# Two hybrid attention layers on one core: TensorE order written by hand, heads alternating, value products in long runs

## The chip, the cores and the metric

One core of one Trainium2 chip runs the whole program in one launch. The metric is device time in microseconds (us): the median of several executions. One execution was also profiled, and its trace is what is read below.

TensorE does the matrix products (in the profile PE, its weight loads PEld), VectorE is DVE, ScalarE is ACT, GpSimd is POOL, and SyncE (SP) issues the weight transfers.

## What is computed

A block of sequence length 256 and width 1024, all in float32: a retention/mLSTM mixer, a feed-forward layer and a gated embedding; a sparse attention mixer, a second feed-forward layer and gated embedding; and then two hybrid layers with a last norm. The change is in the hybrid layers. Cut to what matters, such a layer is:

```python
def hybrid_layer(x, mod, ...):
    h = rms_norm_2(x, norm_g) * (1 + scale) + shift
    a_qkv, a_z, m_cq, m_ckv, m_kr, m_z, merge = split(h @ w_in)
    y_a = dilated_mixer(a_qkv, rel_bias) * silu(a_z)          # 8 heads of 64, 3 groups, one softmax over the groups
    y_m = mla_mixer(m_cq, m_ckv, m_kr, ...) * silu(m_z)       # 16 heads, causal, keys of 64 + 32 rotary columns
    g_a, g_m = split(sigmoid(merge))
    return x + gate * ((g_a * (y_a @ w_out_a) + g_m * (y_m @ w_out_b)) @ w_o)
```

## The kernel before

The tokens stand in two blocks of 128 (`tb`). Every weight tile (128 x 1024 floats, 512 KB) goes the same way in `wt`: SyncE issues its transfer into a buffer `raw` (5 of them), ScalarE copies it, rounded, to `whi` (L448), VectorE forms the rest `wlo` (L449), and both of these have 4 buffers. A projection is then three products for each piece of 128 rows (`mm3`, L465 to L467): high by high, high by low, low by high. The line numbers of these three stand for nearly all of TensorE's projections. Their sums are built in three PSUM banks (`acc`, pool `pacc`).

A hybrid layer goes through these parts in program order (`hybrid`):

- the narrow projections and the first group's values (`c_part`, `v_part`), then `quad_in(0, (0,))`, the queries and keys of the first group for heads 0 to 3;
- MLA: values of all 16 heads (`vm`, L1517), then `mla_chunk(0..3)`, four heads each: keys, queries, and for each pair of heads the scores (L1556, contracting over 128 rows), softmax and `pv_pair`;
- `quad_in(0, (1, 2))`, then `quad(0)`: the dilated attention of heads 0 to 3, in two pairs `pr`, each head `e` of a pair in turn; `quad_in(1, ...)`, `quad(1)` for heads 4 to 7;
- the gates `silu_gate` of `mz` and `az`, the merge projections `mg` (L1603), and the output projections.

In a quad the scores of one head (L1465) contract over 64 rows. Head `e` of a pair has rows 0 to 63 or 64 to 127 of the array: the profile writes 64*128. For one head the order in the program is: two groups of 256 keys into one PSUM tile (`sc`, 2 buffers), the third group into the next, and, for the first token block, three groups of 128 keys into another. VectorE adds the bias and takes the extreme value in one instruction (L1468), ScalarE exponentiates (L1473), VectorE scales (L1475).

`pv_pair` takes the probabilities of one group and two heads: three 128 x 128 transposes for each head (L677) into `tp`, a copy to a separate tile `pT` (L682 on ScalarE for one head, L680 on VectorE for the other), then the value products: for each head 256 columns (L685) and 128 columns (L688), into 64 of the 128 partitions of `po`; the profile writes 128*64. So one group of one pair has two products at L685 and two at L688, and the trace records each float32 product of these lines as two passes.

The program order is not the order on the engines. A planner takes all instructions when the program is built and gives each engine its own fixed order by dependences, priorities and estimated costs; so TensorE's order mixes heads, stages and projections freely.

## Time and profile before

| what | value |
|---|---|
| median of 3 executions | 1460.59 us (1460.12 to 1461.44) |
| the profiled execution, its own time | 1459.07 us |
| its span, from first to last instruction | 1457.3 us |
| TensorE busy | 1415.5 us, 97% |
| VectorE busy | 1032.6 us, 71% |
| ScalarE busy | 761.8 us, 52% |
| granted TensorE clock, mean | 0.988 of full speed |

A matmul's time in the profile runs from its start to its modelled end, and matmuls are pipelined: busy time says that something was under way, not that the array was full. What one of them costs its successors is read from one start to the next. The MLA part and the quads with their projections lie at 782 to 968 us in the first hybrid layer and at 1133 to 1319 us in the second.

### The profile page before, as it was taken

To read this page: it belongs to the slowest core of one execution; us is meant where nothing else is said; L and a number is where in the kernel's file an instruction comes from. 1 tells how busy PE (TensorE), PEld (TensorE's weight loads), DVE (VectorE), ACT (ScalarE), POOL (GpSimd) and SP (SyncE) were. 2 spreads that over 40 slices of the span, in tenths; PEclk is the share of its full clock that TensorE was granted. 3 is DMA by queue.
4 is the path that set the end of the run, shared out by engine and by line. 5 is a ranking of instruction groups with operands and counts; after the bars stand their busy time and mean duration, and the time that the engine had idled before them with its cause. 6 is when DMAs were issued, how large, how long until landed. Compare 5 with 4: busy or idle time off the path is not lost.

```text
span 1457.3 us, 23812 instructions
## 1 busy us (share of the span) xinstructions
PE 1415.5 (97%) x9011; PEld 1211.7 (83%) x9011; DVE 1032.6 (71%) x2250; ACT 761.8 (52%) x1383; POOL 56.6 (4%) x89
## 2 busy tenths in 40 slices
PE   8999999999999999999989999999999999999997
PEld 7878999887755699997788888988879787989886
DVE  7678698978777788897677754555577865456466
ACT  6355565446455665553656544444455754344553
POOL 0000000003000000000210011000000102000000
PEclk9999999999979999999999999999999999999999
DMA  7445677875630266687543353525554435434561
GB/s 270 137 144 163 185 246 243 325 281 194 231 110 1 75 216 217 216 293 279 185 142 123 127 167 114 179 83 188 193 192 144 139 110 145 141 124 145 188 209 51
DMA packets 74903, 251.89 MB, mean 173 GB/s; under 512 B 10362, under 2 KB 14498, under 8 KB 74660
## 3 DMA queue, kind: packets, MB, share of 16 engines
q1 hardware_dynamic: 68880, 239.87, 49.1%
q0 software_dynamic: 3840, 6.32, 1.7%
q10 hardware_dynamic: 2068, 4.18, 1.1%
q8 instruction: 71, 1.16, 0.3%
q14 instruction: 44, 0.36, 0.1%
HBM read 248.42 MB, written 1.90 MB: 172 GB/s over the span
## 4 chain that ended last, share of the span: by engine, by line
PE 85%; DVE 6%; ACT 3%; DMA 2%; issue 2%; POOL 1%; SPq 0%; ACTq 0%; DVEq 0%; POOLq 0%
PE acc L465 22%; PE acc L467 22%; PE acc L466 22%; PE po L685 4%; PE tp L677 3%; PE sc L1465 2%; PE sc L1178 2%; DVE wlo L449 2%; ACT whi L448 2%; DMA raw<-weights 1%; PE po L688 1%; PE sc L1556 1%; DMA gb<-rows 1%; POOL rs L631 1%; PE tp L577 1%
## 5 line engine op out<-in xcount | busy, mean ns | idle before, releaser
L449 DVE TENSOR_TENSOR wlo<-raw,whi 128x1024 fp32r<-128x1024 f32 (+2 forms) x386 | 460.1, 1196 | 213.7 <-ACT whi L448 211.5
L448 ACT ACTIVATE whi<-raw 128x1024 fp32r<-128x1024 f32 (+2 forms) x386 | 399.1, 1037 | 335.6 <-PE acc L467 180.3
L465 PE MATMUL acc<-xh,whi 128*128 128x256 f32 (+1 forms) x1360 | 386.7, 285 | 7.1 <-ACT xh L581 4.7
L466 PE MATMUL acc<-xl,whi 128*128 128x256 f32 (+1 forms) x1360 | 388.3, 286 | 0.7 <-DVE xl L582 0.7
L467 PE MATMUL acc<-xh,wlo 128*128 128x256 f32 (+1 forms) x1360 | 386.1, 284 | 0.9 <-DVE wlo L449 0.9
L465 PEld LDWEIGHTS acc<-xh,whi 128*128 128x128 f32 (+1 forms) x1360 | 258.8, 191 | 13.3 <-ACT xh L581 5.7
L466 PEld LDWEIGHTS acc<-xl,whi 128*128 128x128 f32 (+1 forms) x1360 | 259.2, 191 | 6.5 <-issue 4.1
L467 PEld LDWEIGHTS acc<-xh,wlo 128*128 128x128 f32 (+1 forms) x1360 | 259.1, 191 | 2.3 <-DVE wlo L449 1.6
L465 PE MATMUL acc<-whi,xh 128*128 128x512 f32 (+2 forms) x688 | 249.6, 364 | 2.2 <-DVE xh L1354 1.2
L467 PE MATMUL acc<-whi,xl 128*128 128x512 f32 (+2 forms) x688 | 249.2, 363 | 1.3 <-DVE xl L582 1.2
L466 PE MATMUL acc<-wlo,xh 128*128 128x512 f32 (+2 forms) x688 | 248.8, 362 | 0.0
L465 PEld LDWEIGHTS acc<-whi,xh 128*128 128x128 f32 x688 | 130.7, 190 | 23.9 <-ACT xh L581 1.9
L467 PEld LDWEIGHTS acc<-whi,xl 128*128 128x128 f32 x688 | 130.4, 190 | 22.3 <-DVE xl L582 2.5
L466 PEld LDWEIGHTS acc<-wlo,xh 128*128 128x128 f32 x688 | 130.8, 190 | 19.2 <-issue 1.7
L465 PE MATMUL acc<-whi,gh 128*128 128x512 f32 x176 | 70.3, 399 | 0.0
L466 PE MATMUL acc<-wlo,gh 128*128 128x512 f32 x176 | 69.5, 395 | 0.0
L467 PE MATMUL acc<-whi,gl 128*128 128x512 f32 x176 | 69.4, 394 | 0.0
L680 DVE COPY pT<-tp 128x384 f32<-128x384 f32 x56 | 31.1, 556 | 42.3 <-PE tp L677 41.3
L682 ACT ACTIVATE pT<-tp 128x384 f32<-128x384 f32 x56 | 27.1, 484 | 53.7 <-PE tp L677 52.2
L677 PE MATMUL tp<-const_g,pr 128*128 128x128 f32 x336 | 54.0, 285 | 0.1
L677 PEld LDWEIGHTS tp<-const_g,pr 128*128 128x128 f32 x336 | 37.2, 143 | 17.1 <-issue 12.0
L605 ACT ACTIVATE sqj<-h 128x512 f32<-128x512 f32 (+1 forms) x44 | 24.3, 552 | 51.7 <-DVE h L1629 20.5
(412 smaller groups left out, 1947.8 us busy)
## 6 DMA issues: line engine op xcount, KB each, us to landing
raw<-weights SPq DMA_DIRECT2D x384, 512.0 KB, 3.8
adw<-weights SPq DMA_DIRECT2D x48, 512.0 KB, 4.9
bias<-brow POOLq DMA_DIRECT2D x48, 128.0 KB, 3.3
w<-weights SPq DMA_DIRECT2D x8, 512.0 KB, 8.4
raw<-weights SPq DMA_DIRECT2D x8, 416.0 KB, 4.6
const_ab<-consts SPq DMA_DIRECT2D x1, 1536.0 KB, 9.9
h<-x SPq DMA_DIRECT2D x4, 256.0 KB, 4.6
gb<-rows ACTq DMA_DIRECT2D x2, 512.0 KB, 5.0
```

Source lines behind the costliest of these rows:

```text
L448: nc.scalar.activation(hi, r, AF.Copy)
L449: nc.vector.tensor_tensor(lo, r, hi.bitcast(F32), op=ALU.subtract)
L465: mm(out, lhsT=a[0], rhs=b[0], start=start, stop=False)
L466: mm(out, lhsT=a[0], rhs=b[1], start=False, stop=False)
L467: mm(out, lhsT=a[1], rhs=b[0], start=False, stop=stop)
L605: self.nc.scalar.activation(j, src, AF.Square, scale=2048.0 ** -0.5, accum_out=dst)
L677: nc.tensor.transpose(tp[:, j * P:(j + 1) * P], a, self.ident)
L680: nc.vector.tensor_copy(pT, tp[:, :384])
L682: nc.scalar.activation(pT, tp[:, :384], AF.Copy)
L685: nc.tensor.matmul(po[e * 64:e * 64 + 64, :], lhsT=v(s, 0, e), rhs=pts[e][:, 0:T], start=start and s == 0, stop=False)
L1178: nc.tensor.matmul(s4, lhsT=qT[hs, pr, tb * P:(tb + 1) * P], rhs=kT[hs, g, :, 0:nk], start=True, stop=True)
L1465: nc.tensor.matmul(s3[:, g - g0], lhsT=qs[g][hs, pr, tb * P:(tb + 1) * P], rhs=ks[g][hs, pr, :nk], start=True, stop=True)
```

## The change

TensorE instructions go through a small class `TensorE`, which, while `pinned` is set, tells the planner to keep them in program order. It is set from the first MLA projection to the end of the second quad in each hybrid layer; the other engines are planned as before. The program order in that stretch is rewritten:

- The scores of a quad's two heads are made together: the loop over groups is outside, that over the two heads inside, each head into its own PSUM bank; the third group's go to two `acc` banks.
- The probabilities of both token blocks of a head lie in one tile (`pr`, 3 x 384, 4 buffers); `turn` transposes them and copies them back into the same place, so `pT` is gone. `cn` and the output tiles of the last norm take buffers of the same tag.
- `pv_all` issues the value products of all groups of a pair (or, in MLA, of both pairs of a chunk) in one run, the heads alternating: first all of 256 columns, then all of 128.
- Projections become generators that yield after half a weight tile (`tr_parts`, `quad_in`, `mg`, `silu_gate`), and `take(fill, n)` puts n such pieces at given places among the attention's parts: `quad_in(0, (1, 2))` among the MLA chunks, the `mz` gates in `quad(0)`, the first `az` gate and merge projections in `quad(1)`. `quad_in(1, ...)` stands alone between the quads.
- The next MLA chunk's keys and queries (`mla_in`) are made between the scores and the value products of the present one, and its queries are summed in `acc` instead of `sc`.
- `raw` has 4 buffers instead of 5, in the whole program.

The core of the diff (removed lines are those of the functions printed above; equal lines left out):

```diff
+class TensorE:
+    def __init__(self, tc):
+        self.tc, self.pinned = tc, False
+    def matmul(self, *a, **k):
+        return self.keep(self.tc.nc.tensor.matmul(*a, **k))
+    def transpose(self, *a, **k):
+        return self.keep(self.tc.nc.tensor.transpose(*a, **k))
+    def keep(self, ins):
+        if self.pinned:
+            self.tc.keep_in_program_order(ins)
+        return ins
...
-        raw = self.wp.tile([P, W], F32, tag="raw", bufs=5, name=self.nm("raw"))
+        raw = self.wp.tile([P, W], F32, tag="raw", bufs=4, name=self.nm("raw"))
...
+        def tr_parts(keys):
+            acc = self.pa.tile([P, 2, T], F32, tag="acc", name=self.nm("acc"))
+            for c2, key in enumerate(keys):
+                w = self.wt((key, 0))
+                for kb in range(8):
+                    self.mm3(acc[:, c2, :], w[kb], (xh[:, kb, :], xl[:, kb, :]), kb == 0, kb == 7)
+                    if kb == 3:
+                        yield
+                if c2 == 0:
+                    yield
+            return acc
...
+        def take(gen, n):
+            for _ in range(n):
+                next(gen, None)
+        def probs():
+            return ph.tile([P, 3, 384], F32, tag="pr", bufs=4, name=self.nm("pr"))
+        def turn(a, on_vector):
+            tp = self.pt.tile([P, 512], F32, tag="tp", name=self.nm("tp"))
+            for j in range(3):
+                self.pe.transpose(tp[:, j * P:(j + 1) * P], a[:, j * P:(j + 1) * P], self.ident)
+            if on_vector:
+                nc.vector.tensor_copy(a, tp[:, :384])
+            else:
+                nc.scalar.activation(a, tp[:, :384], AF.Copy)
+        def pv_all(items):
+            for n, (po, pts, v) in enumerate(items):
+                for e in range(2):
+                    self.pe.matmul(po[e * 64:e * 64 + 64, :], lhsT=v(0, e), rhs=pts[e][:, 0:T], start=n == 0, stop=False)
+            for n, (po, pts, v) in enumerate(items):
+                for e in range(2):
+                    self.pe.matmul(po[e * 64:e * 64 + 64, P:T], lhsT=v(1, e), rhs=pts[e][:, T:384], start=False,
+                                   stop=n == len(items) - 1)
...
+        def quad(qd, fill):
+            def scores(pr):
...
+                ps, bs, nms, ls = [], [], [], []
+                        nc.gpsimd.dma_start(b3[:, g], bass.AP(b0.tensor, b0.offset + ((4 * qd + 2 * pr + e) * 3 + g) * 384 + 127,
...
+                    bs.append(b3)
+                    ps.append(probs())
+                    nms.append(self.sm.tile([P, 3], F32, tag="nm", name=self.nm("nmx")))
+                    ls.append(self.sm.tile([P, 2], F32, tag="l", name=self.nm("l")))
+                for tb, g0, g1, j in ((1, 0, 2, 0), (1, 2, 3, 1), (0, 0, 3, 2)):
+                    nk = P * (tb + 1)
+                    n = (g1 - g0) * nk
+                    if n == T:
+                        sps = [self.pa.tile([P, T], F32, tag="acc", name=self.nm("acc")) for _ in range(2)]
+                    else:
+                        sps = [self.psc.tile([P, 512], F32, tag="sc", name=self.nm("sc"))[:, :n] for _ in range(2)]
+                    sps = [sp.rearrange("p (g k) -> p g k", k=nk) for sp in sps]
+                    if tb == 0:
+                        take(fill, 1)
+                    for g in range(g0, g1):
+                        for e in range(2):
+                            hs = slice(e * 64, e * 64 + 64)
+                            self.pe.matmul(sps[e][:, g - g0], lhsT=qs[g][hs, pr, tb * P:(tb + 1) * P],
+                                           rhs=ks[g][hs, pr, :nk], start=True, stop=True)
+                    o = P * tb
+                    for e in range(2):
+                        p, nm, l = ps[e], nms[e], ls[e]
+                        nc.vector.tensor_tensor_reduce(p[:, g0:g1, o:o + nk], sps[e], bs[e][:, g0:g1, T - nk:], -1.0, 3e38,
+                                                       ALU.add, ALU.min, nm[:, j:j + 1])
+                    for e in range(2):
+                        p, nm, l = ps[e], nms[e], ls[e]
+                        if j == 0:
+                            continue
                         if tb:
                             tt(nm[:, 0:1], nm[:, 0:1], nm[:, 1:2], op=ALU.min)
+                        k = 2 * (1 - tb)
+                        a = p[:, :, o:o + nk]
+                        nc.scalar.activation(a, a, AF.Exp, scale=-1.0, bias=nm[:, k:k + 1], accum_out=l[:, tb:tb + 1])
                         nc.vector.reciprocal(l[:, tb:tb + 1], l[:, tb:tb + 1])
+                        ts(a, a, l[:, tb:tb + 1], None, ALU.mult)
+                return ps
+            def values(pr, ps):
+                for g in range(3):
+                    for e in range(2):
+                        turn(ps[e][:, g], e)
+                    take(fill, 1)
                 po = self.pv.tile([P, T], F32, tag="po", name=self.nm("po"))
+                pv_all([(po, [ps[e][:, g] for e in range(2)],
+                         lambda kb, e, g=g: vs[g][:, kb, (2 * pr + e) * 64:(2 * pr + e + 1) * 64]) for g in range(3)])
                 nc.scalar.activation(oa[:, 2 * qd + pr], po, AF.Copy)
+            a = scores(0)
+            take(fill, 2)
+            b = scores(1)
+            take(fill, 1)
+            values(0, a)
+            take(fill, 1)
+            values(1, b)
         ss = self.sm.tile([P, 2, 2], F32, tag="css2", name=self.nm("css2"))
+        cn = probs()[:, 0:2]
         for tb in range(2):
             nc.scalar.activation(cn[:, tb], acc[tb][:, :384], AF.Copy)
             self.sumsq(ss[:, 0, tb:tb + 1], cn[:, tb, 0:256], 256)
             self.sumsq(ss[:, 1, tb:tb + 1], cn[:, tb, 256:384], 128)
         for j, w in enumerate((256, 128)):
...
-                acc = self.psc.tile([P, 2, T], F32, tag="sc", name=self.nm("sc"))
+                acc = self.pa.tile([P, 2, T], F32, tag="acc", name=self.nm("acc"))
...
+            return kT, qTs
+        def mla_scores(kT, qT, pr):
+            pp = probs()
+            nm = self.sm.tile([P, 2, 2], F32, tag="nm", name=self.nm("nmx"))
+            l = self.sm.tile([P, 2, 2], F32, tag="l", name=self.nm("l"))
+            for tb in (1, 0):
+                nk = P * (tb + 1)
+                sp = self.psc.tile([P, 2, T], F32, tag="sc", name=self.nm("sc"))
+                for e in range(2):
+                    self.pe.matmul(sp[:, e, :nk], lhsT=qT[:, e, tb * P:(tb + 1) * P], rhs=kT[:, 2 * pr + e, :nk],
+                                   start=True, stop=True)
+                p = [pp[:, e, P * tb:P * tb + nk] for e in range(2)]
+                for e in range(2):
+                    nc.vector.tensor_tensor_reduce(p[e], sp[:, e, :nk], mask[:, T - nk:], -1.0, 3e38, ALU.add,
+                                                   ALU.min, nm[:, tb, e:e + 1])
+                    nc.scalar.activation(p[e], p[e], AF.Exp, scale=-1.0, bias=nm[:, tb, e:e + 1],
+                                         accum_out=l[:, tb, e:e + 1])
+                nc.vector.reciprocal(l[:, tb], l[:, tb])
+                for e in range(2):
+                    ts(p[e], p[e], l[:, tb, e:e + 1], None, ALU.mult)
+            return pp
+        def mla_values(cq, pps, fill):
+            for pp in pps:
+                for e in range(2):
+                    turn(pp[:, e], e)
+                take(fill, 1)
+            po = self.pv.tile([P, 2, T], F32, tag="po", name=self.nm("po"))
+            pv_all([(po[:, pr], [pps[pr][:, e] for e in range(2)],
+                     lambda kb, e, h0=4 * cq + 2 * pr: vm[:, kb, (h0 + e) * 64:(h0 + e + 1) * 64]) for pr in range(2)])
+            nc.scalar.activation(om[:, 2 * cq:2 * cq + 2], po, AF.Copy)
+        self.pe.pinned = True
+        qk = mla_in(0)
+        vm = ph.tile([P, 2, D], F32, tag="vm8", name="vm")
+        (vh, vl), = self.wt((f"hy{i}.uv", 0))
+        for c2 in range(2):
+            for tb in range(2):
+                acc = self.pa.tile([P, 512], F32, tag="acc", name=self.nm("acc"))
+                s, f = slice(tb * P, (tb + 1) * P), slice(c2 * 512, c2 * 512 + 512)
+                self.mm3(acc, (ch[:, 2, s], cl[:, 2, s]), (vh[:, f], vl[:, f]), True, True)
+                nc.scalar.activation(vm[:, tb, f], acc, AF.Copy)
+        fill = quad_in(0, (1, 2))
         for cq in range(4):
+            kT, qTs = qk
+            pps = [mla_scores(kT, qTs[0], 0)]
+            take(fill, 2)
+            pps.append(mla_scores(kT, qTs[1], 1))
+            if cq < 3:
+                qk = mla_in(cq + 1)
+            else:
+                take(fill, 2)
+            mla_values(cq, pps, fill)
+            take(fill, 2)
+        for _ in fill:
+            pass
...
         def silu_gate(key, b, src):
+            acc = yield from tr_parts([f"{key}{2 * b}", f"{key}{2 * b + 1}"])
             t = self.wk.tile([P, 2, T], F32, tag="gt", name=self.nm("gt"))
             nc.scalar.activation(t, acc, AF.Tanh, scale=0.5)
             stt(t, t, 1.0, acc, ALU.add, ALU.mult)
             stt(src, t, 0.5, src, ALU.mult, ALU.mult)
+            yield
+        def mz():
+            for b in range(4):
+                yield from silu_gate(f"hy{i}.mz", b, om[:, 2 * b:2 * b + 2])
+        def az(b):
+            return silu_gate(f"hy{i}.az", b, oa[:, 2 * b:2 * b + 2])
+        tm = []
+        def mg():
+            for c4 in range(4):
+                tm.append(ph.tile([P, 2, 512], F32, tag="b4", bufs=4, name=self.nm("tm")))
+                acc = [self.pa.tile([P, 512], F32, tag="acc", name=self.nm("acc")) for _ in range(2)]
+                for kb in range(8):
+                    if kb % 2 == 0:
+                        w = self.wt((f"hy{i}.mg{c4}", kb // 2))
+                    for tb in range(2):
+                        s = slice(tb * P, (tb + 1) * P)
+                        self.mm3(acc[tb], (xh[:, kb, s], xl[:, kb, s]), w[kb % 2], kb == 0, kb == 7)
+                    if kb < 7:
+                        yield
+                for tb in range(2):
+                    nc.scalar.activation(tm[c4][:, tb], acc[tb], AF.Tanh, scale=0.5)
+                yield
+        def chain(*gens):
+            for g in gens:
+                yield from g
+        fill = mz()
+        quad(0, fill)
+        for _ in chain(fill, quad_in(1, range(GROUPS))):
+            pass
+        fill = chain(az(0), mg())
+        quad(1, fill)
+        take(fill, 1)
+        self.pe.pinned = False
+        for _ in chain(az(1), fill):
+            pass
```

## Rows read from the trace of the kernel before

**Rows 1.** The page: busy time of TensorE in the whole span, and the chain that ended last, by engine.

```profile
PE 1415.5 (97%) x9011; PEld 1211.7 (83%) x9011; DVE 1032.6 (71%) x2250; ACT 761.8 (52%) x1383; POOL 56.6 (4%) x89
...
PE 85%; DVE 6%; ACT 3%; DMA 2%; issue 2%; POOL 1%; SPq 0%; ACTq 0%; DVEq 0%; POOLq 0%
```

**Rows 2.** Stretches of both hybrid layers: length, busy us of each engine, PEclk, DMA share, GB/s.

```profile
782.00:862.00 80.00, 78.45 (x584) 69.03 (x584) 54.02 (x158) 48.87 (x115) 3.32 (x6) 1.00 0.44 136
862.00:892.00 30.00, 29.87 (x186) 20.37 (x186) 17.88 (x53) 12.90 (x29) 7.49 (x12) 1.00 0.37 106
892.00:938.00 46.00, 46.00 (x385) 45.94 (x383) 20.61 (x19) 19.35 (x21) 0.00 (x0) 1.00 0.54 172
1133.00:1214.00 81.00, 78.28 (x586) 69.86 (x584) 54.33 (x158) 47.38 (x114) 2.95 (x5) 1.00 0.44 134
```

**Rows 3.** Timeline of TensorE, one head's scores: start us, us, line, out<-in, shape, xcount of passes.

```profile
1289.61 1.56 PE L1465 MATMUL sc<-qk,qk 64*128 64x256 f32 x6
1291.10 0.38 PE L465 MATMUL acc<-xh,whi 128*128 128x256 f32 x1
```

**Rows 4.** Timeline of TensorE, shorter score runs in the first layer's quad.

```profile
870.83 0.71 PE L1465 MATMUL sc<-qk,qk 64*128 64x128 f32 x4
871.47 0.65 PE L685 MATMUL po<-pT,v 128*64 128x256 f32 x2
872.05 0.70 PE L1465 MATMUL sc<-qk,qk 64*128 64x128 f32 x4
872.68 0.88 PE L677 MATMUL tp<-const_g,pr 128*128 128x128 f32 x6
873.49 0.70 PE L1465 MATMUL sc<-qk,qk 64*128 64x256 f32 x2
874.11 0.43 PE L685 MATMUL po<-pT,v 128*64 128x256 f32 x1
```

**Rows 5.** Groups by form of TensorE inside 872.04 to 872.60 us: xcount, busy us, mean ns.

```profile
L1465 PE MATMUL sc<-qk,qk 64*128 64x256 f32 x2 | 0.7, 428 | 0.0
L1465 PE MATMUL sc<-qk,qk 64*128 64x128 f32 x2 | 0.5, 322 | 0.0
```

**Rows 6.** Timeline of TensorE, value products of one MLA pair in a single run.

```profile
831.13 0.65 PE L685 MATMUL po<-pT,vm 128*64 128x256 f32 x4
831.62 0.39 PE L688 MATMUL po<-pT,vm 128*64 128x128 f32 x4
831.94 0.39 PE L467 MATMUL acc<-xh,wlo 128*128 128x256 f32 x1
```

**Rows 7.** Timeline of TensorE, value products of another MLA pair in two runs.

```profile
796.93 0.65 PE L685 MATMUL po<-pT,vm 128*64 128x256 f32 x2
797.51 0.49 PE L1556 MATMUL sc<-kT,mqT 128*128 128x128 f32 x2
797.93 0.43 PE L685 MATMUL po<-pT,vm 128*64 128x256 f32 x1
...
798.72 0.55 PE L677 MATMUL tp<-const_g,pr 128*128 128x128 f32 x3
```

**Rows 8.** Busy TensorE of the quads' score products (L1465) alone, both layers.

```profile
782.00:1458.00 676.00, 38.41 (x192) 23.95 (x192) 1.00 0.46 145
```

**Rows 9.** Busy TensorE of all value products (tile po) alone, both layers.

```profile
782.00:1458.00 676.00, 57.50 (x320) 26.40 (x320) 0.00 (x0) 9.16 (x24) 1.00 0.46 145
```

**Rows 10.** Costliest groups of VectorE over both hybrid layers, by form.

```profile
L449 DVE TENSOR_TENSOR wlo<-raw,whi 128x1024 fp32r<-128x1024 f32 x156 | 190.8, 1224 | 167.6 <-ACT whi L448 165.7 <-PE acc L467 1.9
...
L1584 DVE SCALAR_TENSOR_TENSOR gt<-gt,acc 128x512 f32<-128x512 f32 x12 | 8.2, 680 | 0.0
```

**Rows 11.** Waits of the whole span, longest first: us in total, times, longest us.

```profile
ACT whi L448 <- PE acc L467: 180.3, 109, 4.7
...
ACT whi L448 <- DMA raw<-weights: 12.4, 9, 3.8
```

**Rows 12.** DMA issues of the bias rows: KB each, median us to landing.

```profile
bias<-brow POOLq DMA_DIRECT2D x48, 128.0 KB, 3.3
```

More of the change, by code (lines that the diff above doesn't have):

```diff
@@ L456, in wraw @@
         if raw is None:
-            raw = self.wp.tile([P, W], F32, tag="raw", bufs=5, name=self.nm("raw"))
+            raw = self.wp.tile([P, W], F32, tag="raw", bufs=4, name=self.nm("raw"))
         o = OFFS[key]
@@ L1321, in ada @@
                 ps = self.pt.tile([P, 512], F32, tag="tp", name=self.nm("tp"))
-                nc.tensor.matmul(ps, lhsT=self.ones, rhs=acc[:, c * 512:(c + 1) * 512], start=True, stop=True)
+                self.pe.matmul(ps, lhsT=self.ones, rhs=acc[:, c * 512:(c + 1) * 512], start=True, stop=True)
                 nc.scalar.activation(self.gbc[i][:, c * 512:(c + 1) * 512], ps, AF.Copy)
@@ L1421, in quad_in @@
                 for n, lst in enumerate((qs, ks)):
-                    acc = self.tr([f"hy{i}.{'qk'[n]}{qd}{g}{c2}" for c2 in range(2)], xs)
+                    acc = yield from tr_parts([f"hy{i}.{'qk'[n]}{qd}{g}{c2}" for c2 in range(2)])
                     t = dt("qk")
@@ L1592, in split @@
             return hl
-        for b in range(4):
-            silu_gate(f"hy{i}.mz", b, om[:, 2 * b:2 * b + 2])
         ym = split(om, 8)
-        for b in range(2):
-            silu_gate(f"hy{i}.az", b, oa[:, 2 * b:2 * b + 2])
-        tm = [ph.tile([P, 2, 512], F32, tag="b4", bufs=4, name=self.nm("tm")) for _ in range(4)]
-        for c4 in range(4):
-            acc = self.nat(f"hy{i}.mg{c4}", xs, 8)
-            for tb in range(2):
-                nc.scalar.activation(tm[c4][:, tb], acc[tb], AF.Tanh, scale=0.5)
         ya = split(oa, 4)
```

156 lines of the change are left out of this document (48 added, 108 removed).

## Prediction, made before the change was run

> **What bounds the kernel now.** I read the page first: TensorE is under way for 97% of the span and holds 85% of the chain that ended last [rows 1]. Then the stretches of the hybrid layers: from 782 to 938 us it is busy 154 of 156 us, VectorE in the same stretches 54.0 of 80, 17.9 of 30 and 20.6 of 46 [rows 2]. So only less TensorE work, or the same work in less time, can shorten these layers; its waits are small (1.6 us in the first layer's MLA stretch, 2.7 us in the second's). The granted clock was 1.00 there, the upper of its two levels, so there is no clock term.
>
> Next I asked what TensorE does with that time. A projection costs 46.0 / 385 = 0.12 us from one start to the next [rows 2], and the change leaves their number alone. The attention's own products are dearer. One head's six passes of 256 columns take 1.49 us, start to next line's start [rows 3]; two passes take 0.62 [rows 4]. So a pass costs (1.49 - 0.62) / 4 = 0.217 us, and entering and leaving such a run 0.62 - 2 x 0.217 = 0.19 us. Four passes of 128 columns take 0.64 [rows 4], so one costs 0.11.
>
> Now the row that decides. The run at 872.05 is also four passes [rows 4], but the view by form shows two of 256 and two of 128 [rows 5]: products of different lengths, which in this program belong to different heads. It took 0.63 us, what the two long passes cost alone. The second head's passes were free: rows 0 to 63 and 64 to 127 work at once. The value products show the same for column halves: one group of a pair in one run takes 0.81 us (831.13 to 831.94) [rows 6]; serially its passes would need 4 x 0.217 + 4 x 0.11 = 1.31. Cut in two runs, with another head's work between, the same eight passes take 0.58 + 0.79 = 1.37 us [rows 7]. The planner seldom puts both heads side by side: the quads' scores sum to 38.4 us [rows 8] and the value products to 57.5 [rows 9].
>
> **Scores.** There are 8 pairs (2 layers, 2 quads, 2 pairs): 38.4 / 8 = 4.80 us each now. In the changed order each array half gets three products of 256 columns in one run (6 passes: 6 x 0.217 + 0.19 = 1.49) and, after a projection piece, three of 128 (6 x 0.11 + 0.19 = 0.85). That is 2.34 us, or 18.7 in all: 19.7 us less. Ends: with no overlap at all a pair costs 12 x 0.217 + 12 x 0.11 + 0.38 = 4.3 us, and the gain is 4 us; the upper end is the 19.7. I take the upper, since the row at 872.05 is the same operation with the same operands' shape. MLA's scores (L1556) contract over 128 rows and gain nothing.
>
> **Value products.** 24 groups in the quads and 16 MLA pairs make 40 groups: 57.5 / 40 = 1.44 us each. In a long run a group costs each half 2 x 0.217 + 2 x 0.11 = 0.65, and the run 0.81 - 0.65 = 0.16 once. Eight quad runs of three groups and eight MLA runs of two: 40 x 0.65 + 16 x 0.16 = 28.6 us, a gain of 28.9. Ends: nothing, if the runs behave like the cut ones [rows 7]; 28.9. I take 27.
>
> Both sums take it that the halves work side by side from the first pass to the last. If a product's two passes are issued one behind the other and no later one may start first, only the neighbours of two heads overlap, and each run lasts one pass longer: 8 x (0.217 + 0.11) + 16 x 0.217 = 6 us less gain. The run of [rows 6] would then take five slots, 3 x 0.217 + 2 x 0.11 + 0.16 = 1.03 us; it took 0.81, so I leave this out of the sum. [...]
>
> **What is moved or unchanged.** Transposes, their copies on ScalarE and VectorE, softmax and projections keep their numbers; the copies only go to another place. The values of all heads (`uv`) now stand between the first MLA queries and scores, where TensorE waited: of the 4.3 us idle in the two MLA stretches I take 3 back (ends 0 and 4.3).
>
> **`raw` with 4 buffers.** SyncE's transfers now wait for the tile four back instead of five. ScalarE's rounding waits mainly for TensorE to free `whi` (180 us) and only 12.4 us, nine times, for a transfer [rows 11]; so tiles mostly land early and one buffer less is covered by that lead. Where they already wait, at layer starts, each wait can grow by about one tile's turn, 24 projections or 2.9 us: 9 x 2.9 = 26 us of ScalarE, most of it ahead of TensorE. Ends 0 and 10; I take 3.
>
> **New waits.** With the order pinned, TensorE stands still when the next instruction's input is late, and everything behind it stands too; before, another head or projection could have been planned there. The input is VectorE's. In the changed quad TensorE has 4.7 us of scores, twelve transposed heads at about 0.4 (six transposes take 0.81, [rows 4]) = 4.8, 2 x 2.1 of value products and 12 pieces of 12 projections = 17.3: 31 us. VectorE has the 17.9 us that it spends in today's quad [rows 2], plus six weight splits of 1.22 and three gates of two operations of 0.68 [rows 10]: 17.9 + 7.3 + 4.1 = 29.3. That fits, with 2 us to spare, but the needs are not even: TensorE reaches the second pair's transposes after some 22 us, and by then VectorE must have done both pairs' softmax, half the copies, 4 to 5 splits and two gates, about 23.5 us, having started a microsecond late. So I take 2.5 us a quad, 10 in all (ends 0 and 8 a quad). The bias rows [rows 12] of the second pair's second head wait for a buffer of the first pair, as before, and land 3.3 us after issue; that falls within the 5 us of pieces and scores between them, and I add nothing. An MLA chunk is 18 us of TensorE (six pieces 8.6, the next chunk's 30 projections 3.6, scores 8 x 0.217 + 8 x 0.11 = 2.6, transposes 1.6, value products 1.5); VectorE's load for MLA with its two groups (54.0 us [rows 2]) stays below these 4 x 18 = 72 us. Its transposes come 6 to 8 us behind the scores. I take 0.5 us a chunk, 4 in all (ends 0 and 3 each), which includes the queries now sharing three `acc` banks with an unfinished piece.
>
> **The sum.** -19.7 - 27 - 3 + 3 + 10 + 4 = -33 us. The profiled execution took 1459.1 us (1.8 beside its span) and would take 1426.4; the median is 1.5 us above it, so I predict 1427.5 us.
>
> **Rivals.**
>
> - VectorE hands half of it back. For: 29 of 31 us in a quad is nearly a full engine, and every TensorE microsecond saved makes it fuller. Against: it averages 68% in the MLA stretch. With 2.5 us at each of 8 pairs and 2 at each of 8 chunks, 36 us of waits instead of 14: 1449 us. [...] Chance 0.17.
> - The heads do not overlap in the scores as I read them, while the value products do: 16 us less gain, 1443 us. Against it is the run of 0.63 us. Chance 0.07.
> - Slower: the pinned order meets a VectorE queue that the planner has sorted by wrong estimates, with weight splits ahead of the softmax. A split is 1.22 us; two or three of them ahead at each of 16 first transposes are 3 us each, 48 us, and from there nothing is left of the gain. At 4.5 us each it is 1427.5 - 14 + 72 = 1485 us. For it: the planner fills TensorE well now because it may choose. Chance 0.08, and 0.03 for ending within 0.2%.
> - Passes in strict order, as worked out above: 1433 us. Chance 0.1.
> - Better: no new waits at all, 1413 us. Chance 0.1.
>
> My forecast has the remaining 0.45, with its own range from 1416 to 1440. From the better case to the first rival the range is 1408 to 1449. Differences under 0.2% (3 us) are about what a measurement of this kernel cannot tell from no change. Faster 0.89, same 0.03, slower 0.08.
>
> **What would show it.** In the profile after: L1465 alone near 19 us busy, value products near 30, six-pass runs of two heads near 1.5 us with both heads' forms in them; the stretch from the first MLA scores to the second quad's end shorter by some 20 us a layer; TensorE waits at L677's successor naming VectorE or ScalarE copies. Wrong would make me: score runs lasting twice that; VectorE over 90% busy through a whole quad with TensorE waiting several microseconds per pair; or ScalarE waiting for `raw` in the first 740 us.

## The result, and the profile after

The changed kernel takes 1424.3 us (median of 4 runs, 1421.5 to 1426.8) against 1461.0 for the kernel before beside it: a ratio of 0.9745, 95% interval 0.9722 to 0.9768, so 37 us faster. Its profiled execution took 1421.5 us, with a span of 1419.7.

The page of the changed kernel, busy time and the chain that ended last (compare [rows 1]):

```profile
PE 1367.4 (96%) x9011; PEld 1193.7 (84%) x9011; DVE 1032.7 (73%) x2250; ACT 759.1 (53%) x1375; POOL 54.9 (4%) x89
...
PE 80%; DVE 10%; DMA 3%; ACT 3%; issue 3%; POOL 1%; SPq 0%; DVEq 0%; ACTq 0%; POOLq 0%
```

As many TensorE instructions as before, and 48.1 us less busy time (1415.5 to 1367.4). The span fell by 37.6. So the engine's idle time, span less busy, rose from 41.8 to 52.3 us: 48 us of work gone, 10.5 us of it given back as waits. VectorE's work is what it was (1032.6 and 1032.7), and its share of the chain went from 6% to 10%.

Three kinds of products lost the time. All matmuls are recorded at one line now (L380), so they are found by tile: the scores by `qk`, the value products by `po`, MLA's scores by `mqT`. Windows of both hybrid layers, changed kernel; the columns are stretch, length, busy us of PE, PEld, DVE and ACT, then PEclk, DMA share, GB/s (the last row has PE alone):

```profile
735.00:1420.00 685.00, 21.95 (x192) 15.74 (x192) 8.26 (x12) 6.96 (x12) 0.99 0.49 153
735.00:1420.00 685.00, 29.54 (x320) 19.87 (x320) 0.00 (x0) 7.86 (x16) 0.99 0.49 153
735.00:1420.00 685.00, 23.49 (x128) 0.99 0.49 153
```

Scores went from 38.41 [rows 8] to 21.95 us, value products from 57.50 [rows 9] to 29.54. MLA's scores, which I expected to stay, went from 26.2 to 23.49; their group in the kernel before:

```profile
L1556 PE MATMUL sc<-kT,mqT 128*128 128x256 f32 (+1 forms) x128 | 26.2, 334 | 1.2 <-DVE mqT L1545 1.2
```

Together 47.1 us of the 48.1. How it came about is seen in the timeline of TensorE in the first layer, changed kernel: a pair's long scores, its short ones, the short ones of the quad's second pair, a pair's value products, an MLA chunk's. The line after a run is the next instruction, whose start ends it (after the third run it starts at 869.94):

```profile
858.11 1.13 PE L380 MATMUL sc<-qk,qk 64*128 64x256 f32 x8
859.08 0.60 PE L380 MATMUL acc<-qk,qk 64*128 64x256 f32 x4
859.61 0.39 PE L380 MATMUL acc<-xh,whi 128*128 128x256 f32 x1
...
861.23 0.94 PE L380 MATMUL sc<-qk,qk 64*128 64x128 f32 x12
862.09 0.39 PE L380 MATMUL acc<-xh,whi 128*128 128x256 f32 x1
...
868.36 0.48 PE L380 MATMUL sc<-qk,qk 64*128 64x128 f32 x2
869.08 0.93 PE L380 MATMUL sc<-qk,qk 64*128 64x128 f32 x10 [0.23 <-DVE nmx L1541]
...
879.92 2.17 PE L380 MATMUL po<-pr,v 128*64 128x256 f32 x24
882.02 0.39 PE L380 MATMUL acc<-xh,whi 128*128 128x256 f32 x1
...
802.96 1.52 PE L380 MATMUL po<-pr,vm 128*64 128x256 f32 x16
804.41 0.39 PE L380 MATMUL acc<-xh,whi 128*128 128x256 f32 x1
```

Twelve long passes take 859.61 - 858.11 = 1.50 us: what six took for one head before [rows 3]. Twelve short ones take 0.86 in the first pair of each quad, a quad's value run 2.10, an MLA run 1.45. I had worked out 1.49, 0.85, 2.11 (three groups of 0.65 and 0.16) and 1.46. In the trace's start times the passes come in pairs, 5 to 7 ns apart, and behind the first pair the next ones of long passes follow 0.22 us apart.

In the second pair of each quad the twelve short passes take longer: 869.94 - 868.36 = 1.58 us here, 1.40 to 1.61 in the four quads. Head 1's `sc` bank still holds long scores that VectorE has not reduced, and most of the run stands until that is done (868.32 + 0.69 = 869.01):

```profile
868.32 0.69 DVE L1541 CUSTOM_DVE_ANT_0 pr<-sc,bias 128x512 f32<-128x512 f32 x1
```

The four runs sum to 6.1 us where four of 0.87 would be 3.5, so this costs 2.7 us; the view of waits below counts only 0.7 of it as idle time, since two passes of head 0 run meanwhile.

And the waits, TensorE in both hybrid layers of the changed kernel (us in total, times, longest):

```profile
PE tp L383 <- DVE pr L1493: 6.3, 8, 1.2
PE tp L383 <- DVE cl L600: 4.8, 2, 2.4
PE acc L380 <- DVE mqT L1630: 3.3, 4, 1.0
...
PE sc L380 <- DVE nmx L1541: 0.7, 3, 0.3
```

The first is a quad's transposes, twice in each of the four quads: there are two `tp` banks, and a head can be transposed only into one whose last head has been copied out. The second stands ahead of the rotary keys' transposes (`krs`) and so of the first MLA queries, once a layer. The third is the second query sum of an MLA chunk, which needs an `acc` bank while a half-finished piece holds another.

The two waits of the first pair in the first quad, changed kernel: TensorE (in brackets the idle time before, and what ended it), then ScalarE, then VectorE:

```profile
874.97 0.87 PE L383 MATMUL tp<-const_g,pr 128*128 128x128 f32 x6 [1.24 <-DVE pr L1493]
...
878.01 0.55 PE L383 MATMUL tp<-const_g,pr 128*128 128x128 f32 x3 [0.41 <-DVE pr L1493]
```

```profile
874.00 0.60 ACT L1551 ACTIVATE pr<-pr,nmx 128x384 f32<-128x384 f32 x1
...
874.60 0.47 ACT L1495 ACTIVATE pr<-tp 128x384 f32<-128x384 f32 x1
```

```profile
874.38 0.54 DVE L1493 COPY pr<-tp 128x384 f32<-128x384 f32 x1
...
875.89 1.20 DVE L467 TENSOR_TENSOR wlo<-raw,whi 128x1024 fp32r<-128x1024 f32 x1
877.02 0.48 DVE L1553 TENSOR_SCALAR pr<-pr,l 128x384 f32<-128x384 f32 x1
877.41 0.54 DVE L1493 COPY pr<-tp 128x384 f32<-128x384 f32 x1
```

The view puts both down to VectorE, and the times agree: its copies end at 874.38 + 0.54 = 874.92 and 877.41 + 0.54 = 877.95, just ahead of the starts at 874.97 and 878.01. Its first copy stands behind the second pair's reductions and scaling, the second behind a weight split and another scaling. ScalarE is hardly earlier: its copy at 874.60, behind the second pair's exponentials, ends at 875.07, when the first of the six transposes already run, so it would have held the others up had VectorE been in time.

```profile
862.00:892.00 30.00, 28.09 (x244) 25.04 (x240) 23.03 (x52) 17.47 (x34) 7.46 (x12) 1.00 0.50 145
```

Yet over 30 us of this quad (columns PE, PEld, DVE, ACT, POOL) VectorE is busy 23.0 (17.9 in the same 30 us before, [rows 2]), ScalarE 17.5, and TensorE idle 1.9. The copies are late at a moment; no engine is overloaded.

### The profile page after: what moved, and what is told of

It is laid out like the page before. It is cut to its first block, busy times and chain, and to the rows that moved or that the text cites. A ratio compares the mean times of both kernels' runs of the same rounds, so it can differ in the third digit from the quotient of the medians.

```text
span 1419.7 us, 23788 instructions
## 1 busy us (share of the span) xinstructions
PE 1367.4 (96%) x9011; PEld 1193.7 (84%) x9011; DVE 1032.7 (73%) x2250; ACT 759.1 (53%) x1375; POOL 54.9 (4%) x89
## 4 chain that ended last, share of the span: by engine, by line
PE 80%; DVE 10%; DMA 3%; ACT 3%; issue 3%; POOL 1%; SPq 0%; DVEq 0%; ACTq 0%; POOLq 0%
PE acc L380 67%; PE sc L380 4%; PE po L380 4%; PE tp L383 3%; DVE wlo L467 3%; DMA raw<-weights 2%; PE tp L380 2%; ACT whi L466 1%; DVE pr L1553 1%; DVE pr L1541 1%; DMA bias<-brow 1%; DMA gb<-rows 0%; DVE mt L648 0%; DVE h L984 0%; ACT sqj L623 0%
## 5 line engine op out<-in xcount | busy, mean ns | idle before, releaser
L467 DVE TENSOR_TENSOR wlo<-raw,whi 128x1024 fp32r<-128x1024 f32 (+1 forms) x386 | 460.7, 1196 | 202.4 <-ACT whi L466 201.7
L466 ACT ACTIVATE whi<-raw 128x1024 fp32r<-128x1024 f32 (+1 forms) x386 | 399.7, 1037 | 350.3 <-PE acc L380 296.7
L380 PE MATMUL acc<-xh,whi 128*128 128x256 f32 (+1 forms) x1360 | 389.9, 288 | 7.3 <-ACT xh L599 3.7
L380 PE MATMUL acc<-xl,whi 128*128 128x256 f32 (+1 forms) x1360 | 386.1, 284 | 0.3 <-DVE xl L600 0.3
L380 PE MATMUL acc<-xh,wlo 128*128 128x256 f32 (+1 forms) x1360 | 385.2, 284 | 1.2 <-DVE wlo L467 1.1
L380 PEld LDWEIGHTS acc<-xh,whi 128*128 128x128 f32 (+1 forms) x1360 | 258.9, 191 | 14.2 <-ACT xh L599 4.8
L380 PEld LDWEIGHTS acc<-xh,wlo 128*128 128x128 f32 (+1 forms) x1360 | 259.2, 191 | 2.6 <-DVE wlo L467 1.8
L380 PEld LDWEIGHTS acc<-xl,whi 128*128 128x128 f32 (+1 forms) x1360 | 259.5, 191 | 1.9 <-DVE xl L600 1.2
L380 PE MATMUL acc<-whi,xh 128*128 128x512 f32 (+2 forms) x688 | 252.2, 368 | 1.9 <-DVE xh L1372 1.2
L380 PE MATMUL acc<-whi,xl 128*128 128x512 f32 (+2 forms) x688 | 248.7, 363 | 1.6 <-DVE xl L600 1.6
L380 PE MATMUL acc<-wlo,xh 128*128 128x512 f32 (+2 forms) x688 | 248.0, 361 | 0.0
L380 PEld LDWEIGHTS acc<-whi,xh 128*128 128x128 f32 x688 | 130.5, 190 | 24.9 <-issue 2.5
L380 PEld LDWEIGHTS acc<-whi,xl 128*128 128x128 f32 x688 | 130.1, 189 | 22.8 <-DVE xl L600 2.9
L380 PEld LDWEIGHTS acc<-wlo,xh 128*128 128x128 f32 x688 | 130.5, 190 | 18.7 <-issue 1.7
L380 PE MATMUL acc<-whi,gh 128*128 128x512 f32 x176 | 70.3, 399 | 0.0
L380 PE MATMUL acc<-wlo,gh 128*128 128x512 f32 x176 | 69.5, 395 | 0.0
L380 PE MATMUL acc<-whi,gl 128*128 128x512 f32 x176 | 69.4, 394 | 0.0
L1324 DVE CUSTOM_DVE_ANT_0 adw<-adw,ada 128x1024 f32<-128x1024 f32 x32 | 39.1, 1223 | 15.7 <-DMA adw<-weights 15.4
L1516 POOL DMA_DIRECT2D bias<-brow x48 | 29.5, 637 | 527.2 <-DVE l L1552 159.9
```

The source lines that it names most:

```text
L380: return self.keep(self.tc.nc.tensor.matmul(*a, **k))
L466: nc.scalar.activation(hi, r, AF.Copy)
L467: nc.vector.tensor_tensor(lo, r, hi.bitcast(F32), op=ALU.subtract)
L1324: nc.vector.tensor_tensor_reduce(raw, raw, cr, 1.0, 0.0, ALU.mult, ALU.add, m[:, j:j + 1])
L1516: nc.gpsimd.dma_start(b3[:, g], bass.AP(b0.tensor, b0.offset + ((4 * qd + 2 * pr + e) * 3 + g) * 384 + 127, [[24 * 384 - 16, 8], [24 * 384 ...
```

## The experiments

Medians in us, ratios to the kernel before, measured beside each, with their 95% intervals.

| kernel | median | ratio |
|---|---|---|
| changed | 1424.3 | 0.9745 (0.9722 to 0.9768) |
| s1: score heads one after another inside a run | 1427.3 | 0.9771 (0.9756 to 0.9786) |
| s2: value heads one after another inside a run | 1427.1 | 0.9778 (0.9763 to 0.9793) |
| s3: not pinned | 1416.5 | 0.9701 (0.9688 to 0.9714) |
| s4: before, `raw` with 4 buffers | 1459.6 | 0.9993 (0.9985 to 1.0002) |
| u1: scores in two runs by head | 1428.1 | 0.9769 (0.9748 to 0.9790) |
| u2: value products in two runs by head | 1453.6 | 0.9942 (0.9927 to 0.9957) |
| u12: both | 1458.3 | 0.9973 (0.9961 to 0.9984) |
| t12: pinned, two waits covered | 1419.1 | 0.9707 (0.9691 to 0.9723) |
| v1: pinned, quads' copies on ScalarE | 1422.3 | 0.9729 (0.9710 to 0.9749) |
| b3: not pinned, pieces moved, one more piece | 1414.4 | 0.9684 (0.9659 to 0.9709) |
| b4: b3 without the one more piece | 1412.3 | 0.9670 (0.9645 to 0.9695) |
| b5: b3 with the quads' copies on ScalarE | 1411.3 | 0.9652 (0.9633 to 0.9671) |

**s1 and s2, only the order inside a run.**

```diff
-                    for g in range(g0, g1):
-                        for e in range(2):
+                    for e in range(2):
+                        for g in range(g0, g1):
```

s2 swaps the two loops of `pv_all` in the same way.

> Changed kernel, with the two heads of a score run one after another again (all products of rows 0 to 63, then all of rows 64 to 127); order, pieces between, and value products as in the changed kernel. Theory 1, the gain is two array halves working at once: in the changed kernel a run of 12 long passes takes 1.50 us and one of 12 short ones 0.87; one after another they take 12 x 0.217 + 0.19 = 2.8 and 12 x 0.11 + 0.19 = 1.5, which over 8 pairs is 8 x (4.3 - 2.4) = 15 us more TensorE time; some of it falls where TensorE waits for VectorE today (9 us in the four quads), so 8 to 15 us slower than the changed kernel, near 1435. Rival, the gain is the written order with projections between and fewer, longer runs: score runs no longer than now, within 3 us of the changed kernel.

> Changed kernel, with the two heads of a value run one after another (per column block, all products of output rows 0 to 63, then all of rows 64 to 127); all else as in the changed kernel. Theory 1, column halves work at once: a quad's run of 24 passes goes from 2.10 us to 12 x 0.217 + 12 x 0.11 + 0.16 = 4.1, an MLA run of 16 from 1.45 to 2.8, so 8 x 2.0 + 8 x 1.35 = 27 us more, less what the change of heads inside the run still overlaps: 22 to 27 us slower, near 1448. Rival, the gain is in the length of the runs and the order: within 3 us of the changed kernel.

Both came out some 3 us slower (their intervals overlap the changed kernel's), where I had expected 8 to 15 and 22 to 27: a miss for my reading of what alternation does. The timeline of TensorE in s1, the same runs as above:

```profile
860.75 1.14 PE L380 MATMUL sc<-qk,qk 64*128 64x256 f32 x8
861.72 0.60 PE L380 MATMUL acc<-qk,qk 64*128 64x256 f32 x4
862.25 0.39 PE L380 MATMUL acc<-xh,whi 128*128 128x256 f32 x1
...
863.88 1.26 PE L380 MATMUL sc<-qk,qk 64*128 64x128 f32 x12
865.07 0.39 PE L380 MATMUL acc<-xh,whi 128*128 128x256 f32 x1
```

The long run still takes 1.50 us, although the program now has head 0's two products ahead of head 1's first. The passes' starts still come in pairs, 13 ns apart. Only the short runs of the first pairs, with three products of one head in a row, became longer (1.19 here, for 0.86). s2's MLA runs, two products of a head in a row, take 1.50 for 1.45, its quad runs with three in a row 2.58 for 2.10. So in these runs products of the other half started ahead of some that precede them in the program; the times are put together in the last section. The swap is no test of whether the halves overlap; they must be taken apart.

**u1, u2 and u12, the heads in separate runs.** As many pieces as in the changed kernel, one of them now between the heads' runs. u1 has as many score runs as the changed kernel, by head instead of by length; u2 has one more value run each (in the last MLA chunk of a layer no piece is left, and both heads' products stand in one run).

```diff
 # u1, scores(pr)
+for e in range(2):
+    if e:
+        take(fill, 1)
+    for tb, g0, g1, j in ((1, 0, 2, 0), (1, 2, 3, 1), (0, 0, 3, 2)):
+        ...   head e's products alone, three banks
+    ...       then head e's reductions and softmax
 # u2, pv_all
+for e in range(2):
+    if e:
+        take(fill, 1)
     for n, (po, pts, v) in enumerate(items):
-        for e in range(2):
```

> Changed kernel, but a pair's scores in two runs by head instead of by length: head 0's six products, the projection piece, head 1's six products. As many runs, pieces and products as in the changed kernel; what goes is that both heads' products stand in one run, so no two row halves can work at once. (Swapping the heads inside a run had cost only 3 us, since the long runs still showed pairs starting 13 ns apart.) Theory 1, the halves working at once is the gain: a run takes 6 x 0.217 + 6 x 0.11 + 0.19 = 2.15 us, a pair 4.3 where the changed kernel takes 1.50 + 0.87 and its wait; 8 x 1.7 to 1.9 = 13 to 15 us more, 10 to 15 slower than the changed kernel with the waits that this covers: 1434 to 1440. Rival, the gain is long runs in a written order: as many runs, so within 3 us of the changed kernel.

> Changed kernel, but the value products in two runs by head: head 0's products of all groups, one projection piece (taken from behind), head 1's. Nothing else moves; column halves can no longer work at once. Theory 1: a quad's head takes 6 x 0.217 + 6 x 0.11 + 0.16 = 2.12 us, as much as both heads take in the changed kernel (2.10), an MLA head 4 x 0.327 + 0.16 = 1.47 (both now: 1.45); 8 x 2.1 + 8 x 1.5 = 29 us more, near 1453. Rival, long runs and order are the gain: one more run each, 16 x 0.17 = 3 us.

Value products of one head in u2, from the timeline of TensorE, and all of them in the windows of both layers:

```profile
887.02 2.16 PE L380 MATMUL po<-pr,v 128*64 128x256 f32 x12
889.12 0.39 PE L380 MATMUL acc<-xh,whi 128*128 128x256 f32 x1
```

```profile
735.00:1420.00 685.00, 57.67 (x320) 37.97 (x320) 0.00 (x0) 7.85 (x16) 0.99 0.48 150
```

One head takes 2.10 us, as long as both take together in the changed kernel; the sum of 57.67 is that of the kernel before [rows 9]. The time rose by 29.3 us, to 1453.6: the whole of it shows. Theory 1 holds, and the rival (3 us) falls.

Scores in u1 double as foreseen, but the time does not. Timeline of TensorE, then the windows of `qk`:

```profile
860.53 1.13 PE L380 MATMUL sc<-qk,qk 64*128 64x256 f32 x4
861.49 0.59 PE L380 MATMUL acc<-qk,qk 64*128 64x256 f32 x2
861.93 0.83 PE L380 MATMUL sc<-qk,qk 64*128 64x128 f32 x6
862.68 0.39 PE L380 MATMUL acc<-xh,whi 128*128 128x256 f32 x1
```

```profile
735.00:1420.00 685.00, 35.63 (x192) 29.80 (x192) 8.28 (x12) 6.96 (x12) 0.99 0.49 153
```

A head takes 862.68 - 860.53 = 2.15 us, the scores 35.63 us for 21.95: 13.7 us more work. The time is 1428.1, only 3.8 more than the changed kernel (the two intervals overlap). u1's view of waits, and its window of the same 30 us, show where the rest went. The view still has `cl` (4.8 us) and `mqT` (3.3), and no row for a quad's copies or reductions:

```profile
862.00:892.00 30.00, 30.00 (x237) 27.86 (x236) 23.63 (x60) 16.28 (x32) 7.11 (x12) 1.00 0.49 143
```

The waits for the copies (6.3 us) and reductions (0.7) are gone; TensorE is busy in all 30 us. VectorE and ScalarE had the same work and more time for it, and were nowhere late there. (They also get head 0's scores before head 1's, which no run separates from the slower products.) So of the score products' gain about 7 us by the view of waits was handed straight back in the quads. Counted from start to start, the sixteen runs take 16 x 2.16 = 34.6 us in u1 and would take 8 x (1.50 + 0.87) = 19.0 in the changed kernel with no bank late: 15.6 less. Of this the late bank takes 2.7 and the copies some 7.6, an estimate: each of the eight waits is about 0.16 us longer so counted, since a product (0.28 us) is followed by the next after 0.12. That leaves 5.3 us, which fits the times: within one kernel they follow the mean granted clock (the changed kernel took 1421.5 us at 0.988 and 1426.8 at 0.985), and at the same clock u1 is 4 to 5 us behind it (1431.4 against 1426.8 at 0.985, 1428.6 against 1424.0 and 1424.6 at 0.986).

> Both undone together: scores in runs by head and value products in runs by head, a projection piece between; pinned order, transposes in place, pieces and the moved work stay as in the changed kernel. If the parts add up, it is slower than the changed kernel by what each cost alone, 4 + 29 = 33 us, near 1457, and only 4 us of the whole gain belong to the rest (order, pieces, moved work). Rival, the parts hide one another: the value runs give VectorE the time that it lacks in the quads, so the scores' 13 us of TensorE time show in full, 29 + 13 = 42, near 1466, slower than the kernel before.

1458.3: the parts add up (3.8 + 29.3 = 33.1; measured 34.0), and the rival's 1466 falls. On top of u2 the scores cost 4.7 us, as on top of the changed kernel. What is left to order, pieces and moved work is 3.4 us against the kernel before (2.3 to 5.7 by the ratio's interval); the work in it includes scores of 35.6 us for 38.4 and MLA's scores of 23.5 for 26.2.

**s4, the buffers alone**, in the kernel before.

```diff
-        raw = self.wp.tile([P, W], F32, tag="raw", bufs=5, name=self.nm("raw"))
+        raw = self.wp.tile([P, W], F32, tag="raw", bufs=4, name=self.nm("raw"))
```

> Kernel before, with 4 buffers for raw weight tiles in place of 5 and nothing else. My prediction took 3 us more for it (ends 0 and 10): 1463 to 1464 against 1460.6. Rival, from the traces of the two kernels, whose layers before the hybrid ones end at the same time: transfers land early enough, 0, and only ScalarE's waits for transfers grow (12.4 us in nine waits before).

1459.6 against 1460.5 for the kernel before beside it: nothing. Its row of the waits:

```profile
ACT whi L448 <- DMA raw<-weights: 16.3, 16, 2.9
```

ScalarE waits for a transfer 16 times instead of nine [rows 11], 3.9 us more in all, and its lead ahead of TensorE swallows it.

**s3, not pinned.**

```diff
-        self.pe.pinned = True
+        self.pe.pinned = False
```

> Changed kernel without the pinned stretch: the planner orders TensorE's instructions everywhere, from the same program. My forecast holds that heads and column halves side by side bring the gain, whoever orders them; if the planner keeps the runs whole, the time stays within 8 us of the changed kernel (1416 to 1432), and up to 13 us of waits for VectorE (9 in the quads, 4 in MLA) may partly go, since the planner may choose another instruction. Rival, that only the pinned order keeps the heads side by side: the runs fall apart again and most of the 37 us is lost, 1445 or more.

1416.5 us, 8 less. The planner keeps the runs whole (1.50, 0.87, 2.10 and 1.45 us, value products 29.54 busy). Its waits in both layers:

```profile
PE tp L383 <- DVE pr L1493: 5.5, 8, 1.2
PE acc L380 <- ACT ch L599: 3.2, 2, 1.6
...
PE acc L380 <- DVE kT L1619: 0.5, 1, 0.5
```

MLA's bank waits went from 3.3 to 0.5, and the one ahead of the first queries from 4.8 to 3.2: there the planner had something else to issue. In the quads it had not (5.5 for 6.3). So the pin is not what brings the gain; it costs 8 us, of which the two profiled executions show 4.6 as idle time (52.3 us, and 1415.6 - 1367.9 = 47.7 in s3).

**t12 and v1, two cures under the pin.**

```diff
 # t12
             b = scores(1)
-            take(fill, 1)
+            take(fill, 2)
 # t12, mla_in, for the second query sum (j = 1)
-                acc = self.pa.tile([P, 2, T], F32, tag="acc", name=self.nm("acc"))
+                pool, tag = ((self.pa, "acc"), (self.psc, "sc"))[j]
+                acc = pool.tile([P, 2, T], F32, tag=tag, name=self.nm(tag))
 # v1, values
-                        turn(ps[e][:, g], e)
+                        turn(ps[e][:, g], False)
```

> Changed kernel, still pinned, with two of its waits covered: one more projection piece ahead of the first transposes of a quad (they wait 1.4 to 1.5 us there for VectorE, four times), and the second query sum of an MLA chunk in an sc bank instead of acc (waits of 1.24 and 1.06 us in four chunks). Theory 1, these are waits of the pinned order on the path: 4 x 1.4 + 4.4 = 10 us faster at most; I expect 6 to 10, 1414 to 1418. Rival, VectorE is the bound of these stretches and only hands the wait on: 0 to 3 us faster.

> Changed kernel, still pinned, with the quads' copies of transposed heads all on ScalarE (half of them were VectorE's; MLA's stay). Theory, that VectorE's queue sets the waits ahead of the quads' transposes (1.4 to 1.5 and 0.7 us, four times): VectorE loses 24 copies of 0.55 us, and TensorE gets the banks back sooner; half of the 9 us or more goes, 3 to 8 us faster, 1416 to 1421. Rival, the softmax of the second pair must come first anyway, or ScalarE becomes late in its place: within 2 us.

t12 is 5 us faster, just short of the 6 that I had as the least. Its waits name `mqT` no longer, but the quads' transposes still wait, now for both copiers:

```profile
PE tp L383 <- ACT pr L1495: 3.2, 4, 0.8
PE tp L383 <- DVE pr L1493: 2.2, 4, 0.5
```

That is 5.4 us for 6.3. So most of what was gained should be MLA's bank; the extra piece in the quads bought little, as the rival said. v1's 2 us lie inside the intervals: the second wait of each first pair is gone, and the first stays, now put down to ScalarE's copy behind the exponentials:

```profile
PE tp L383 <- ACT pr L1495: 4.9, 4, 1.3
```

So the larger part of what I took for VectorE's delay in the quads does not go with its copies: whichever engine copies has the second pair's softmax first in its queue.

**b3, b4 and b5, the cures without the pin.** Four pieces of `quad_in(0, (1, 2))` go ahead of the rotary keys' transposes, where TensorE waited, and pieces of `mz` and `mg` take their places later; b3 and b5 also have t12's extra piece, b5 also v1's copies.

```diff
+        qin = quad_in(0, (1, 2))
+        take(qin, 4)
         kp = self.pt.tile([P, 2, T], F32, tag="tp", name=self.nm("tp"))
...
-        fill = quad_in(0, (1, 2))
+        fill = chain(qin, mz())
```

> Planner's order (nothing pinned), one more piece ahead of a quad's first transposes as above, and four projection pieces taken from the MLA stretch and put where TensorE waits 1.9 us a layer before the first MLA queries (gate pieces take their place in the last chunk). If each wait is on the path: 4 x 1.3 + 2 x 1.9 = 9 us less than without the pin alone (1416.5), near 1408. Rival, VectorE is late by as much later on: 1414 to 1417.

> As the best so far (1414.4: planner's order, four pieces moved ahead of MLA, one more piece ahead of a quad's transposes), without that one more piece. In the pinned kernel the waits ahead of these transposes only went from 2.2 to 1.9 us with it, so I expect 0 to 2 us more; if it was worth its whole length, 4 us more or above.

> The best so far (1414.4) with the quads' copies of transposed heads all on ScalarE. If VectorE's queue sets what waits are left in the quads (0.7 to 1.2 us before the scores and transposes of each), 2 to 5 us faster, 1410 to 1412; if ScalarE becomes late in its place, none.

b4 is 4.2 us faster than s3 (the ends of their intervals overlap), and its view of waits has no row for `cl` or `ch` left: the moved pieces cover that wait. Part of the 4.2 us may be the clock: three of b4's four executions had a mean granted clock of 0.989 to 0.990 (1410.7 to 1412.5 us) and the fourth 0.986 (1416.7), while s3 took 1416.1 to 1417.4 at 0.987 to 0.989. The extra piece buys nothing again (b3 is no faster than b4). b5 is the fastest, 1411.3 us: 13 less than the changed kernel, whose waits above come to 15, though its interval overlaps b3's and b4's. It waits 1.6 us in all for the copies.

## Why the prediction was right, and where its steps were off

I predicted 1427.5 us (the terms, added to the tenth, give 1427.9), and the kernel takes 1424.3. The mechanism was the one foreseen: two heads side by side in the array, with part of the gain handed back as waits. By its two halves the sum was close: 46.7 us less work was foreseen (19.7 and 27) and 48.1 found; 14 us more idle (3, 10 and 4 less 3) and 10.5 found. That the total is so close is in part luck: MLA's scores (2.7 us less work than foreseen) and `raw` (3 us not needed) made up for the scores' work (3.2 more) and a wait that I had not foreseen (3.7).

- **Value products: right.** 28.6 us of work foreseen, 29.54 found; u2 gives the term as 29.3 us. The 27 that I took, a little under what the durations gave, was needless caution.
- **Scores: the mechanism right, the net too large.** 18.7 us foreseen, 21.95 found, of which 2.7 is the late `sc` bank of the second pairs. With the quads' waits (10 foreseen; from start to start some 7.6 for the copies beside those 2.7) I counted 9.7 us net; u1 and u12 measure 4 to 5, against scores by head, which themselves take 2.8 us less than in the kernel before. The row at 872.05 was read rightly, but not for the reason given: one head too has products of both lengths, and u1 shows those one after another (2.15 us); what tells is the 0.63 us. The rival that half is handed back came true for this one part, by VectorE's copies with ScalarE's close behind, and for none of the rest: its 36 us of waits, and 1449, did not appear. With scores of 21.95 us TensorE waits 6.3 us for the copies in the quads; with u1's scores of 35.63 these waits are gone.
- **`raw`: mis-sized.** I took 3 us and it costs none (s4).
- **The idle start of MLA: failed, by a wait elsewhere.** I took 3 us back, since `uv` now stands between the first queries and the scores. There it does what I expected: the two waits for `mqT` (1.2 us, in the line of L1556 above) are gone. But in the kernel before `uv` had filled another gap. While VectorE still made `cl`, the low part of MLA's latent, TensorE began the products of `uv` (512 columns) that need only the high part, `ch`, and the rotary keys' transposes came behind them; it stood still for 0.6 us a layer:

```profile
779.27 0.50 PE L465 MATMUL sc<-ch,whi 128*128 128x256 f32 x2 [0.58 <-ACT ch L581]
779.64 0.50 PE L465 MATMUL acc<-whi,ch 128*128 128x512 f32 x1
...
780.45 0.60 PE L1506 MATMUL tp<-const_g,krs 128*128 128x128 f32 x4
```

In the changed kernel these transposes come first, they wait for `cl`, and all MLA products are pinned behind them: 2.4 us a layer. That is 3.7 us more in both, which no term of the sum has. Without the pin it is 1.6 a layer (s3), and moved projection pieces fill it (b4).
- **MLA's waits: right in size.** 4 us foreseen; 3.3 by the view of waits, for the cause that I named, `acc` banks shared with an unfinished piece; t12's view has lost just this row, and most of its 5 us should be that; no run changes the bank alone.
- **MLA's scores: missed.** "Gain nothing" was wrong by 2.7 us of busy time. In u12, with neither score nor value heads side by side, they take 23.50, so heads side by side are not the cause; probably it is that other products no longer stand between them, but nothing here tests that alone.
- **The slower rival, a pinned order behind a badly sorted VectorE queue,** has its mechanism in the trace (a weight split ahead of the copy at 877.41, and of the second pair's reductions), at 0.4 and 0.7 us there, not 4.5.
- **Strict order of passes: refuted,** and not just by the 0.81 us of [rows 6]. In s1's long run head 1's first pass could start no earlier than head 0's fourth, at 3 x 0.217, and its own fourth at 6 x 0.217; the third group's two passes of head 0 would start at 6 and 7, those of head 1 at 7 and 8 times 0.217. With 0.19 the run would last 9 x 0.217 + 0.19 = 2.14 us; it took 1.50.

## What to carry to other kernels

When two heads use half the array each, put their products into one run: here the second head's added next to nothing (twelve long score passes of two heads took 1.50 us, six of one head 1.49 before, [rows 3]), and two products of the same head in a row cost at most 0.05 us a run (s1, s2), three 0.33 and 0.48. Count work and waits apart: the value products, with nothing of VectorE's due behind them, kept all of their gain (29.3 us by u2), and the scores, whose results VectorE must reduce at once, gave about two thirds back (4 to 5 us of 13.7 were left). Write the program in the order that keeps the runs whole, but try it without pinning: here the fixed order turned late copies and occupied banks into idle time, 52.3 us in all where the planner's order had 47.7, and cost 8 us (s3).

## What the runs showed of the hardware that was not expected

Products for the other array half started ahead of products that precede them in the program. With two products of one head in a row the runs took as long as with the heads alternating, or nearly: 1.50 us for 1.50 in s1's long score runs, 1.50 for 1.45 in s2's MLA value runs. With three in a row they took 1.19 for 0.86 in a short score run of s1, and 2.58 for 2.10 in a quad's value run of s2, where the heads in separate runs take 2 x 2.10 = 4.20 (u2). In s1's long run, with four passes of head 0 ahead, head 1's first pass starts 13 ns after head 0's first: three passes of head 0 had not yet started, and a product of head 0 was half done, so it is not a matter of the planner's order, which places whole products. How many products can be overtaken, no run shows.

After the first layer's wait ahead of the MLA queries the granted clock fell from 1.00 to 0.50. Timeline and windows of the changed kernel (PE, PEld, DVE, ACT, POOL, then PEclk):

```profile
779.89 0.88 PE L383 MATMUL tp<-const_g,krs 128*128 128x128 f32 x4 [2.42 <-DVE cl L600]
...
781.21 0.41 PE L380 MATMUL acc<-ch,whi 128*128 128x256 f32 x1
781.43 0.41 PE L380 MATMUL acc<-cl,whi 128*128 128x256 f32 x1
```

```profile
781.00:782.00 1.00, 1.00 (x6) 1.00 (x6) 0.93 (x2) 0.07 (x1) 0.69 (x2) 0.50 0.73 295
...
784.00:785.00 1.00, 1.00 (x11) 1.00 (x11) 0.75 (x2) 1.00 (x2) 0.00 (x0) 1.00 0.98 229
```

At 0.50 (PEclk in the first row) a product follows the last after 0.22 us instead of 0.12. From these transposes to the start of the sixteenth product behind them it took 3.8 us, and 2.3 in the second layer, where the same wait of 2.42 us left the clock at 1.00: about 1.5 us lost. So the first layer's wait cost more than its length and the second's did not; why, no run shows. Of the two levels that the prediction speaks of, the trace of the kernel before shows both: a PEclk of 0.50 from 420 to 439 us, and the 1.00 of [rows 2].
